# Odd sequences' weighted values in two float32r parts, first pages asked for early, one pipeline for both MLPs, and four branch steps moved to ScalarE

## The chip, the cores and the metric

The kernel runs on one core of a Trainium2 chip. The metric is the device time of one execution in microseconds (us). Engines are called as in the profile: PE (TensorE, the matmuls; PEld are its weight loads), DVE (VectorE), ACT (ScalarE), POOL (GpSimd) and SP (SyncE, which here issues the DMAs).

## The reference, cut to what matters

One inference step of a two-layer decoder with width 1024, for a prompt of 1024 tokens and for 8 sample sequences of 4 new tokens (32 columns), which makes 1056 columns in all. Layer 0 runs two branches side by side, stick-breaking attention of 8 heads and an RG-LRU recurrence over 512 channels. Layer 1 is dilated window attention of 16 heads. Behind each mixer stands a squared-ReLU MLP (1024 to 4096 and back).

```
z = u @ w_in                                   # layer 0: q, k, v, xr, g
attn = stick_breaking(q, [past_k; k], [past_v; v])      # samples: 1024 cached keys, 8 pages of 128
xc = conv_b + sum(conv_w[j] * shifted(xr, j) for j in range(4))
a, inp = gates(xc)                             # sigmoid gates, exp and sqrt(1 - a^2) of 128x1056 tiles
h = scan(a, inp);  lru = gelu(g) * h
x = x + [attn, lru] @ w_out
x = x + square(relu(norm(x) @ w_ff1)) @ w_ff2
```

For a sample sequence b the attention ends in `o[b] = sum over pages of weights(32 x 128) @ values(128 x 512)`: 32 rows are 8 heads by 4 tokens, 512 columns are 8 heads of 64, and of each row only its own head's 64 columns are kept.

## The kernel before, in words

Activations lie transposed, 128 channels by 1056 columns, in 8 tiles. A float32 product is mostly made of float32r parts: `x = xh + xl`, `w = wh + wl`, three matmuls (`mm3`). The high part is an ACT copy, the low part a subtraction on DVE or POOL. Weights pass through `raw_w` (a DMA into one of three `ws` buffers), two ACT copies of half a tile each, and one POOL subtraction.

The stages, in us of the profiled span: loading and turning of x, the branch (`lru_phase`) with its projections up to about 210, layer 0's attention by pairs of heads with the next pair's projections between, from about 430 the sample sequences beside the last pair's attention and an early part of the output projection, from 656 the output projection, the first MLP from 740 to 1470, layer 1's attention to about 2200 and its output projection, the second MLP from 2262 and the final norm.

In the branch, in the rest of layer 0's set-up and in the second MLP a scheduler of the language decides the order. The attention stages are written out by a planner: `interleave` takes the next piece of several generators whose inputs are ready by a model of the engines (`Clock`, `Timed`), in which a DMA is charged by its bytes at 360 GB/s. `after` puts a step (a copy, a subtraction, a DMA) at a planned time. Since helpers record the operations, all ACT, DVE, POOL and SP work has line L138, matmuls L213 and transposes L219; operations are told apart by their tiles.

`sb_samples` (L1436) serves the sample sequences. `fetch` asks for one page of 128 keys or values (256 KB) into one of 18 `u` tiles, and four pages are kept asked for. First 64 key pages are turned on PE (`ktr`), split, and scored. Then `spread` turns the weights into tiles `x` of 128 keys by 32 rows. For each sequence 8 pages and the new keys (`wn`, `vs32`) are summed by plain float32 matmuls of 32 weight columns by 512 value columns; `join` turns the result and copies the kept columns into `ats`. In the profile these products read `tr<-u,x`.

The first MLP (`first_mlp`, L1264) runs 64 units of weights, each loaded four units ahead and split two units ahead, all by hand. The second (`finish_layer`, L1213) writes the same sums plainly, with `last_weights` for its last four tiles, and `last_pass` ends in the final norm.

Of the kernel before, what the change touches and what calls it, by code (L numbers as in the profile page):

```python
# [21 lines left out]
NS = 32  # L22
# [14 lines left out]
def f32(ap):  # L37
    return ap.bitcast(F)
# [89 lines left out]
class Timed:  # L128
# [47 lines left out]
class Trunk:  # L176
# [154 lines left out]

    def parts_w(self, kb, cols, pool=None, bufs=4):
        return [(pool or self.wp).tile([128, kb, cols], R, name=self.nm("w"), tag="w", bufs=bufs) for _ in range(2)]

# [303 lines left out]
    def lru_conv(self, f, xr, oc, T):  # L638
# [19 lines left out]
    def lru_block(self, f, g, xc, bd, sp4, tiny, oc, T):  # L658
# [350 lines left out]
    def layer0(self, st, rstd):  # L1009
# [4 lines left out]
        with self.pool("smp0") as sp, self.pool("qkv0") as qkv:  # L1014
# [7 lines left out]
            with self.pool("pair0") as pool:  # L1022
# [52 lines left out]
                def load_lru(k):  # L1075
# [6 lines left out]
                                 k_step, v_step, T, False, done, 2)  # L1082
                proj = self.projections(st, rstd, win, 512, pps, T)
                self.low_queries(T)
                with self.manual():
                    self.interleave((proj, 1))
                    for p in range(4):
                        self.split_pair(pps[p], T, False)
                        if p == 0:
                            self.after(60000, self.states_out, oc, TS("ot", shape=(36, LRU)), need=[oc])  # L1090
                        if p < 3:
                            self.interleave((att, 106.6 if p else 85.8), (proj, 76))
                    sample = self.sb_samples(smp, pps[3], ats, T, x, load, lambda: first.append(
                        self.out_w(self.i["w_out_ab"][0], range(4), 0, 9000)))
                    early = self.early_out(0, self.i["w_out_ab"][0], ops, range(4, 8),
# [117 lines left out]
    def finish_layer(self, l, ops, wsrc, ks, w):  # L1213
# [7 lines left out]
        with self.pool(f"mlp{l}") as hp:  # L1221
# [9 lines left out]
            nx = {}  # L1231
            if l == 0:
                self.first_mlp(st, rstd, w1, w2, h, nx)
                return nx
            for g in range(8):
                th = [hp.tile([128, NT], R, name=self.nm("th"), tag="th", bufs=6) for _ in range(4)]
                tl = [hp.tile([128, NT], R, name=self.nm("tl"), tag="tl", bufs=6) for _ in range(4)]
                for f in range(4):
                    c0 = (g * 4 + f) * 128
                    w = self.weights(w1[:, :, c0:c0 + 128], 8, 128)  # L1240
                    if g == 7 and f == 3:
                        last = self.last_weights(w2)

                    def ev(ps, s, f=f):
                        t = hp.tile([128, CW], F, name=self.nm("t"), tag="t", bufs=3)
                        q = hp.tile([128, CW], F, name=self.nm("t2"), tag="t2", bufs=3)
                        nc.vector.scalar_tensor_tensor(t, ps, 0.0, rstd[:, s], op0=OP.max, op1=OP.mult)
                        nc.scalar.activation(q, t, AF.Square)
                        nc.scalar.activation(th[f][:, s], q, AF.Copy)
                        nc.vector.tensor_sub(tl[f][:, s], q, f32(th[f][:, s]))  # L1250
                    for _ in self.project(st, w, ev):
                        pass
                if g == 7:
                    self.last_pass(last, th, tl, h)
                    break
                for m2 in range(4):
                    w = self.weights(w2[:, g * 4:g * 4 + 4, m2 * 256:(m2 + 1) * 256], 4, 256)
                    for _ in self.contract(w, (2 * m2, 2 * m2 + 1), range(4), th, tl, h):
                        pass
        return nx  # L1260

    def first_mlp(self, st, rstd, w1, w2, h, nx):  # L1264
        nc, hp = self.nc, self.hp
        todo = self.caches(hp)
        raw, parts = {}, {}
# [27 lines left out]
        load(3)  # L1295
        next(todo)
        with self.tc.manual_schedule(engines={getattr(mybir.EngineType, e) for e in
                                              ("PE", "SP", "Pool", "Activation", "DVE")}):
            for u in range(64):
                g, x = divmod(u, 8)  # L1300
# [7 lines left out]
                if x < 4:  # L1308
                    for c in range(3):
# [15 lines left out]
                        if c < 2:  # L1325
                            cut(u + 2, c)
                    continue
                step = self.norm_done(h, self.g[:, 1], nx) if g == 7 else None
# [18 lines left out]
            for _ in todo:  # L1347
                pass
        self.norm_finish(nx)


    def last_weights(self, w2):
        nc, hp = self.nc, self.hp
        ws = []
        for j in range(4):
            src = w2[:, 28:32, j * 256:(j + 1) * 256]
            if j in (0, 3):
                ws.append(self.weights(src, 4, 256))
                continue
            s, a, b = (hp.tile([128, NT], d, name=self.nm("w"), tag=t, bufs=n)[:, :1024].rearrange(  # L1360
                "p (k f) -> p k f", k=4) for d, t, n in ((F, ("acc", "sq")[j - 1], j), (R, "th", 6), (R, "tl", 6)))
            nc.sync.dma_start(s, src)
            self.split_w(s, a, b)
            ws.append((a, b))
        return ws

# [69 lines left out]
    def sb_samples(self, smp, pp, ats, T, x, load, ahead):  # L1436
# [23 lines left out]
        for _ in range(4):  # L1460
            fetch()
        for t in pp["split_s"]:
            t.run()
# [80 lines left out]
        def spread(half, ready):  # L1544

            yield 0, [ready]
            ready.run()
            ws = [x(t, F, (128, 4, 4, 32)) for t in ("xh", "xl")]
            ws.append(T("wn", shape=(NS, 1, 4, 32), bufs=2))
            for j in range(3):  # L1550
# [6 lines left out]
                nc.scalar.activation(ws[j], ps[:m, :n].rearrange("p k (b r) -> p k b r", b=4), AF.Copy)  # L1557
                self.drop(ps)
                yield 0, 0
            return ws  # L1560

        def join(b, o):

            v = u(F, (32, 512))
            nc.vector.transpose(v, o)
            self.drop(o)
# [28 lines left out]
        for t in pp["vlo"]:  # L1595
            t.run()
        for b in range(8):
            half = b // 4
            yield 0, [TR]
            o = turn([32, 512])  # L1600
            for kb in range(9):
                m = 128 if kb < 8 else NS
                yield 0, [ws[half][kb // 4]] + (here[:1] if kb < 8 else [])
                v = here.pop(0) if kb < 8 else smp["vs32"]
                self.mm(o, ws[half][kb // 4][:m, kb % 4, b % 4], v, start=kb == 0, stop=kb == 8)
                if kb < 8:
                    self.drop(v)
                    fetch()
                    yield 0, 0
                if b * 9 + kb == 12:  # L1610
                    ws[1] = yield from spread(1, ready[1])
# [467 lines left out]
```

## Time and profile before

| what | value |
|---|---|
| median of 3 runs | 3019.85 us (3018.76 to 3021.5) |
| the profiled execution, its own time | 3023.94 us |
| span of its trace | 3022.2 us |
| PE busy in the span | 2873.6 us (95%) |
| DVE, ACT, POOL busy | 1666.2, 1222.1, 952.6 us |
| DMA, mean over the span | 141 GB/s |

The span runs from the first instruction to the last; 1.7 us of the profiled execution lie outside it. PE is busy nearly throughout, so time is to be found where it is idle, where its granted clock is below 1.00, and in matmuls that take long for what they do.

### The profile page before, as it was taken

Reading aid. Unit: us, or ns where it says so; the run is one execution under the profiler, and the core shown is the slowest. Engines: PE = TensorE matmul, PEld = TensorE weight load, DVE = VectorE, ACT = ScalarE, POOL = GpSimd, SP = SyncE. Lnnn points to the kernel's source line nnn. Section 1 sums busy time; section 2 is a strip of 40 time slices with the busy share of each in tenths; the row PEclk is TensorE's granted clock in tenths of the full one; section 3 lists DMA queues with packets and bytes.
Section 4 is the critical chain, followed back from the end, with each engine's and each line's share of the span. In section 5 each row is a group of like instructions: output and inputs, shape, how many; then the busy total and the mean of one; then the engine's idle time right before and its main releaser. Section 6 shows DMA issues by size and latency. Waiting matters only on the chain.

```text
span 3022.2 us, 49205 instructions
## 1 busy us (share of the span) xinstructions
PE 2873.6 (95%) x18608; PEld 2730.8 (90%) x18608; DVE 1666.2 (55%) x3597; ACT 1222.1 (40%) x2441; POOL 952.6 (32%) x591
## 2 busy tenths in 40 slices
PE   7889889999999999999999999998989999999998
PEld 6778879659999999999999989997889999999998
DVE  5877897544444444442467878866663332333335
ACT  4455676434343333332455555544342221212222
POOL 2445562123333333341432222223132121212122
PEclk9999999999999999999999999999989999999999
DMA  5111136664877778861355656566531111111111
GB/s 174 43 50 30 43 106 224 191 211 138 253 247 246 252 252 254 258 222 40 131 185 161 216 160 212 158 221 195 169 128 43 49 43 49 43 49 43 50 36 65
DMA packets 366725, 426.16 MB, mean 141 GB/s; under 512 B 23878, under 2 KB 292822, under 8 KB 366488
## 3 DMA queue, kind: packets, MB, share of 16 engines
q1 hardware_dynamic: 366488, 423.01, 43.7%
q8 instruction: 147, 2.41, 0.3%
q14 instruction: 90, 0.74, 0.1%
HBM read 296.23 MB, written 126.17 MB: 140 GB/s over the span
## 4 chain that ended last, share of the span: by engine, by line
PE 73%; DVE 11%; DMA 4%; ACT 4%; issue 4%; POOL 1%; SPq 1%; ACTq 0%; POOLq 0%; DVEq 0%
PE mm L213 58%; PE tr L213 9%; PE tr L219 3%; PE pv L213 2%; DMA ws<-in_w_in_c_dram 1%; DVE u L138 1%; DVE sa L138 1%; DVE w L138 1%; DVE xl L138 1%; DVE f L138 1%; DVE sb L138 1%; ACT w L138 1%; ACT u L138 1%; DMA U<-kv 1%; DVE tl L138 1%
## 5 line engine op out<-in xcount | busy, mean ns | idle before, releaser
L213 PE MATMUL mm<-xh,w 128*128 128x352 f32 x5184 | 1337.0, 329 | 24.8 <-DVE xr L138 7.1
L213 PEld LDWEIGHTS mm<-xh,w 128*128 128x128 f32 x5184 | 926.7, 191 | 34.8 <-DVE xr L138 8.4
L138 POOL TENSOR_TENSOR w<-ws,w 128x1024 fp32r<-128x1024 f32 (+1 forms) x188 | 464.4, 2471 | 1290.1 <-ACT w L138 1194.5
L213 PE MATMUL mm<-xl,w 128*128 128x352 f32 x2592 | 844.8, 326 | 2.8 <-DVE xl L138 2.8
L213 PE MATMUL mm<-th,w 128*128 128x352 f32 (+2 forms) x3072 | 742.0, 323 | 6.1 <-DVE h L138 6.1
L213 PEld LDWEIGHTS mm<-th,w 128*128 128x128 f32 x3072 | 532.7, 188 | 8.9 <-DVE h L138 8.4
L213 PEld LDWEIGHTS mm<-xl,w 128*128 128x128 f32 x2592 | 495.7, 191 | 6.8 <-DVE xl L138 3.1
L213 PE MATMUL mm<-tl,w 128*128 128x352 f32 (+2 forms) x1536 | 493.3, 321 | 0.0
L138 ACT ACTIVATE w<-ws 128x512 fp32r<-128x512 f32 (+1 forms) x376 | 220.3, 616 | 560.1 <-issue 265.1
L138 DVE TENSOR_TENSOR h<-mm,h 128x352 f32<-128x352 f32 (+2 forms) x384 | 200.3, 523 | 417.4 <-PE mm L213 417.4
L213 PEld LDWEIGHTS mm<-tl,w 128*128 128x128 f32 x1536 | 288.6, 188 | 0.0
L138 ACT ACTIVATE u<-tr 128x512 fp32r<-128x512 f32 (+5 forms) x362 | 188.3, 530 | 189.0 <-PE tr L219 151.5
L138 ACT ACTIVATE t<-t 128x352 f32<-128x352 f32 x192 | 95.2, 496 | 412.4 <-DVE t L138 412.4
L138 DVE TENSOR_TENSOR tl<-t,th 128x352 fp32r<-128x352 f32 x192 | 151.3, 788 | 192.6 <-ACT th L138 192.6
L138 DVE SCALAR_TENSOR_TENSOR t<-mm,rstd 128x352 f32<-128x352 f32 x192 | 100.5, 523 | 281.8 <-PE mm L213 276.9
L138 DVE TENSOR_TENSOR u<-tr,u 128x512 fp32r<-128x512 f32 (+3 forms) x272 | 164.0, 612 | 76.2 <-ACT u L138 73.6
L138 POOL TENSOR_TENSOR kvs<-raw,kvs 128x512 fp32r<-128x512 f32 x80 | 103.0, 1295 | 132.7 <-ACT kvs L138 73.8
L213 PE MATMUL pv<-u,v 128*128 128x256 f32 (+1 forms) x736 | 134.3, 298 | 10.7 <-DVE u L138 10.4
L213 PE MATMUL mm<-x,w 128*128 128x352 f32 x720 | 139.8, 333 | 3.7 <-DVE k L138 2.7
L213 PEld LDWEIGHTS pv<-u,v 128*128 128x128 f32 x736 | 107.3, 197 | 21.4 <-DVE u L138 13.3
L213 PEld LDWEIGHTS mm<-x,w 128*128 128x128 f32 x720 | 117.0, 192 | 10.5 <-issue 4.2
L138 DVE TENSOR_TENSOR_SCAN f<-f,ms 128x128 f32<-128x128 f32 (+3 forms) x64 | 100.4, 1569 | 35.6 <-ACT f L138 35.3
(278 smaller groups left out, 3663.6 us busy)
## 6 DMA issues: line engine op xcount, KB each, us to landing
kv<-kvs SPq DMA_DIRECT2D x160, 512.0 KB
U<-kv SPq DMA_DIRECT2D x160, 512.0 KB
ws<-in_w_ff_dram SPq DMA_DIRECT2D x126, 512.0 KB
raw<-in_cache_dil_k_dram SPq DMA_DIRECT2D x320, 64.0 KB
u<-in_cache_sb_k_dram SPq DMA_DIRECT2D x64, 256.0 KB
u<-in_cache_sb_v_dram SPq DMA_DIRECT2D x64, 256.0 KB
raw<-in_cache_dil_v_dram SPq DMA_DIRECT2D x64, 256.0 KB
out_dram<-u SPq DMA_DIRECT2D x48, 256.0 KB
```

What stands on the lines that cost most here:

```text
L138: r = f(*args, **kw)
L213: self.nc.tensor.matmul(out, w, x, start=start, stop=stop)
L219: self.nc.tensor.transpose(out, x, ident)
```

## The change

Five edits, in the diff below.

1. For sequences 1, 3, 5 and 7 weights and values are split into float32r parts. The weights' high and low parts stand side by side as 64 columns, so two matmuls (high values, low values) give all four partial products in 64 rows. `join` adds the two halves of 32 rows. Per odd page there is one ACT copy and one subtraction (22 of 32 on DVE, 10 on POOL). A value page is prepared one page ahead (`got`). The even sequences and the new keys stay in float32.
2. `sb_samples` is made before the last pair of heads but one, and its first step, the four first page DMAs, is planned 145000 PE cycles into that pair's work.
3. The planner charges a DMA at 230 GB/s in place of 360.
4. Both MLPs run the pipeline of the first (`units`); layer 1 stops it at unit 60 and leaves units 60 to 63 to `last_pass`. `last_weights` is gone.
5. In the branch four steps per block on 128x1056 tiles (`xc`, `ge`, `w`, `e`) go from DVE to ACT.

```diff
-                cost = int(np.prod(o.shape)) * 4 / 360 * 2.4
+                cost = int(np.prod(o.shape)) * 4 / 230 * 2.4
...
-        nc.vector.tensor_scalar(xc, xr, cw[3], V[:, 36:37], op0=OP.mult, op1=OP.add)
+        nc.scalar.activation(xc, xr, AF.Identity, scale=cw[3], bias=V[:, 36:37])
...
-        nc.vector.tensor_scalar(ge, ge, 0.044715, 1.0, op0=OP.mult, op1=OP.add)
+        nc.scalar.activation(ge, ge, AF.Identity, scale=0.044715, bias=1.0)
...
-        nc.vector.tensor_scalar_add(w, u, 1.0)
+        nc.scalar.activation(w, u, AF.Identity, bias=1.0)
...
-        nc.vector.tensor_scalar(e, e, 0.25, -1.0, op0=OP.mult, op1=OP.add)
+        nc.scalar.activation(e, e, AF.Identity, scale=0.25, bias=-1.0)
...
+                        if p == 2:
+                            pages = self.after(145000, next, sample)
...
+                    pages.run()
...
-            for g in range(8):
...
-                    w = self.weights(w1[:, :, c0:c0 + 128], 8, 128)
...
+            self.units(l, st, rstd, w1, w2, h, nx)
...
-                parts[u] = self.parts_w(*raw[u].shape[1:], *((hp, 2) if u % 3 == 2 else ()))
+                where = (hp, 4, "wl") if l and u > 61 else (hp, 2) if u % 3 == 2 else ()
+                parts[u] = self.parts_w(*raw[u].shape[1:], *where)
...
-            for u in range(64):
+            for u in range(60 if l else 64):
...
+                    hi, lo = (ws[j][1][..., c:c + 32] for c in (0, 32))
+                    nc.scalar.activation(ws[j][0], src[:, :, 0::2], AF.Copy)
+                    nc.scalar.activation(hi, src[:, :, 1::2], AF.Copy)
+                    lows.append(self.after(300, nc.vector.tensor_sub, lo, src[:, :, 1::2], f32(hi), drops=[ps]))
...
+        def value(n):
+
+            t = here.pop(0)
+            if n // 8 % 2 == 0:
+                return (t,)
+            vh, vl = u(), u()
+            nc.scalar.activation(vh, t, AF.Copy)
+            return vh, vl, self.after(300, (nc.gpsimd if n % 3 == 1 else nc.vector).tensor_sub, vl, t, f32(vh), drops=[t])
...
+            if b % 2:
+                t = u(F, (32, 512))
+                nc.scalar.activation(t, o[32:64], AF.Copy)
+                nc.vector.tensor_add(t, o[0:32], t)
+                nc.vector.transpose(v, t)
...
-                self.mm(o, ws[half][kb // 4][:m, kb % 4, b % 4], v, start=kb == 0, stop=kb == 8)
...
+                if len(v) == 1:
+                    yield 0, [w[kb // 4][0]]
+                    self.mm(o[0:32], lw, v[0], start=n == 0, stop=n == 8)
+                    self.drop(*v)
+                else:
+                    yield 0, [v[2], lows[kb // 4]]
+                    for t in (v[2], lows[kb // 4]):
+                        t.run()
+                    self.mm(o, lw, v[0], start=n == 0, stop=False)
+                    self.mm(o, lw, v[1], start=False, stop=n == 8)
+                    self.drop(*v[:2])
```

DVE's queue in the branch, at the second half of its first block (tiles `w_876`, `e_877`, `a_871`), where the third block's `xr_900` is taken out of PE's banks. Before:

```order
L138 TENSOR_TENSOR xr_900<-mm_909,rstd_290 128x352
L138 TENSOR_SCALAR w_876<-u_849 128x1056
L138 SCALAR_TENSOR_TENSOR e_877<-a_871,w_876 128x1056
L138 TENSOR_TENSOR xr_900<-mm_935,rstd_290 128x352
L138 TENSOR_SCALAR e_877<-e_877 128x1056
L138 TENSOR_TENSOR w_876<-u_849,z_872 128x1056
L138 SCALAR_TENSOR_TENSOR e_877<-a_871,e_877 128x1056
L138 TENSOR_TENSOR z_872<-w_876,z_872 128x1056
L138 TENSOR_TENSOR a_871<-u_849,e_877 128x1056
L138 SCALAR_TENSOR_TENSOR w_876<-z_872,w_876 128x1056
L138 TENSOR_TENSOR xr_900<-mm_961,rstd_290 128x352
```

And now:

```order
L138 TENSOR_TENSOR xr_900<-mm_909,rstd_290 128x352
L138 TENSOR_TENSOR xr_900<-mm_935,rstd_290 128x352
L138 SCALAR_TENSOR_TENSOR e_877<-a_871,w_876 128x1056
L138 TENSOR_TENSOR xr_900<-mm_961,rstd_290 128x352
L138 TENSOR_TENSOR w_876<-u_849,z_872 128x1056
L138 SCALAR_TENSOR_TENSOR e_877<-a_871,e_877 128x1056
L138 TENSOR_TENSOR z_872<-w_876,z_872 128x1056
```

Two steps are gone from the queue, and between the second and the last `xr` stands one long step of the block where six stood before. The second `e` step now waits for a step on ACT.

PE's queue in the value products. Before, in the middle of them (`kb`, `qb`, `sa`, `pv` belong to the last pair's attention):

```order
L213 MATMUL tr_7343<-kb_4091,ql_199_1451 128x512
L213 MATMUL tr_7212<-vs_194_1440,wn_6071 32x512
L213 MATMUL tr_7357<-u_7285,x_6968 32x512
L213 MATMUL tr_7357<-u_7330,x_6968 32x512
L213 MATMUL tr_7357<-u_7336,x_6968 32x512
L219 MATMUL tr_7415<-ident,sa_6966 128x128
L219 MATMUL tr_7415<-ident,sa_7034 128x128 x2
L213 MATMUL tr_7357<-u_7339,x_6968 32x512
L213 MATMUL tr_7357<-u_7364,x_6969 32x512
L213 MATMUL pv_7207<-u_7191,v_1406_5180 128x256
```

Now, where the fourth sequence ends (two rows per odd page) and the fifth begins:

```order
L213 MATMUL tr_7628<-u_7705,x_6152 64x512
L213 MATMUL tr_7628<-u_7706,x_6152 64x512
L213 MATMUL tr_7628<-u_7751,x_6152 64x512
L213 MATMUL tr_7628<-u_7752,x_6152 64x512
L213 MATMUL tr_7628<-vs_194_1440,wn_6153 32x512
L213 MATMUL tr_7628<-u_7759,x_6152 64x512
L213 MATMUL tr_7628<-u_7760,x_6152 64x512
L213 MATMUL tr_7783<-u_7708,wp_7387 32x512
L213 MATMUL tr_7783<-u_7754,wp_7387 32x512
```

The planner has moved the last pair's attention and the early output projection ahead: from the third sequence's second page on, 47 of the 64 value pages follow each other with nothing of the attention between, only the new keys' products, and in the eighth sequence 20 rows of the output projection.

ACT's queue in the second MLP, where the fourth tile of the first group of hidden channels (`th_25912` before, `th_26118` now) is made in three thirds. Before:

```order
L138 ACTIVATE t_6766_26318<-t_26317 128x352
L138 ACTIVATE th_25912<-t_6766_26318 128x352
L138 ACTIVATE w_26447<-ws_26445 128x512 x2
L138 ACTIVATE t_6769_26349<-t_26348 128x352
L138 ACTIVATE th_25912<-t_6769_26349 128x352
```

And now:

```order
L138 ACTIVATE th_26118<-t_6928_26486 128x352
L138 ACTIVATE w_26491<-ws_26258 128x512
L138 ACTIVATE t_6933_26520<-t_26519 128x352
L138 ACTIVATE th_26118<-t_6933_26520 128x352
L138 ACTIVATE w_26491<-ws_26258 128x512
L138 ACTIVATE t_6936_26553<-t_26552 128x352
L138 ACTIVATE th_26118<-t_6936_26553 128x352
```

The two half copies of a weight tile, after which POOL subtracts, stood together ahead of the last third; now one stands behind each of the first two thirds, and the tile is that of two units later.

## Rows read from the trace of the kernel before

**Rows 1.** Stages: window, PE, PEld, DVE, ACT, POOL busy (count), clock, DMA share, GB/s
```profile
97.00:210.00 113.00, 89.67 (x450) 82.30 (x449) 96.89 (x89) 50.87 (x63) 48.70 (x26) 0.89 0.10 34
...
430.00:450.00 20.00, 9.18 (x79) 8.46 (x78) 18.90 (x23) 12.95 (x23) 17.08 (x18) 0.74 0.93 308
...
568.00:656.00 88.00, 87.61 (x257) 26.10 (x255) 36.25 (x70) 26.54 (x49) 16.14 (x15) 1.00 0.69 219
...
740.00:1470.00 730.00, 730.00 (x4556) 729.58 (x4555) 309.84 (x546) 265.29 (x491) 268.29 (x148) 1.00 0.68 219
1470.00:2262.00 792.00, 744.17 (x5292) 701.13 (x5291) 570.52 (x1859) 392.37 (x907) 220.06 (x141) 0.96 0.56 180
2262.00:2990.00 728.00, 721.94 (x4494) 718.15 (x4493) 251.72 (x423) 172.83 (x335) 158.60 (x72) 1.00 0.15 45
```

**Rows 2.** Waits of PE in 97:210, us in total, times, longest
```profile
PE mm L213 <- DVE xr L138: 7.1, 2, 3.7
PE mm L213 <- DVE k L138: 6.4, 2, 5.0
PE mm L213 <- DVE q L138: 3.9, 1, 3.9
PE mm L213 <- DVE g L138: 3.0, 1, 3.0
```

**Rows 3.** Groups of DVE and ACT in 97:210: busy us, mean ns, idle before
```profile
L138 DVE TENSOR_SCALAR w<-u 128x1056 f32<-128x1056 f32 x4 | 6.8, 1688 | 11.7 <-ACT u L138 11.7
...
L138 DVE TENSOR_SCALAR e<-e 128x1056 f32<-128x1056 f32 x4 | 2.8, 701 | 0.0
...
L138 DVE TENSOR_SCALAR xc<-xr,vec 128x1056 f32<-128x1056 f32 x2 | 1.6, 818 | 0.0
...
L138 DVE TENSOR_SCALAR ge<-ge 128x1056 f32<-128x1056 f32 x2 | 1.4, 703 | 0.0
...
L138 ACT ACTIVATE a<-a 128x1056 f32<-128x1056 f32 x4 | 4.3, 1082 | 11.9 <-DVE a L138 11.9
```

**Rows 4.** Timeline at 441: start, us, engine, operation, idle before and its releaser
```profile
441.43 2.48 DVE L138 TENSOR_TENSOR u<-tr,u 128x512 fp32r<-128x512 f32 x4
...
442.22 1.09 PE L219 MATMUL tr<-ident,u 128*128 128x128 f32 x4 [7.63 <-DMA u<-in_cache_sb_k_dram]
```

**Rows 5.** Timeline of PE among the value products; two records are one float32 product
```profile
606.62 2.76 PE L213 MATMUL tr<-u,x 128*32 128x512 f32 x6
609.32 0.50 PE L213 MATMUL tr<-kb,qb 128*128 128x512 f32 x1
609.65 0.40 PE L213 MATMUL tr<-kb,ql 128*128 128x512 f32 x1
609.98 0.61 PE L213 MATMUL tr<-vs,wn 32*32 32x512 f32 x1
```

**Rows 6.** Copies and subtractions of 128x512 tiles in 568:656
```profile
L138 POOL TENSOR_TENSOR x<-u,x 128x512 fp32r<-128x512 f32 x4 | 5.0, 1276 | 18.9 <-ACT x L138 18.9
...
L138 ACT ACTIVATE x<-u 128x512 fp32r<-128x512 f32 x6 | 3.7, 625 | 3.4 <-DMA u<-mix 3.3
...
L138 DVE TENSOR_TENSOR x<-u,x 128x512 fp32r<-128x512 f32 x2 | 1.3, 687 | 0.0
```

**Rows 7.** The fullest ten us of transfers among the value products
```profile
610.00:620.00 10.00, 10.00 (x29) 2.90 (x29) 4.89 (x9) 4.57 (x9) 1.94 (x2) 1.00 0.90 298
```

**Rows 8.** The second MLP, 2262:2990: PE's waits for the sum's evacuation
```profile
PE mm L213 <- DVE h L138: 4.7, 7, 0.9
```

**Rows 9.** Timeline at one of these waits
```profile
2301.45 1.15 ACT L138 ACTIVATE w<-ws 128x512 fp32r<-128x512 f32 x2 [2.14 <-PE mm L213]
...
2302.74 2.40 POOL L138 TENSOR_TENSOR w<-ws,w 128x1024 fp32r<-128x1024 f32 x1 [9.17 <-ACT w L138]
...
2303.56 1.96 DVE L138 TENSOR_TENSOR tl<-t,th 128x352 fp32r<-128x352 f32 x1 [1.47 <-ACT th L138]
```

**Rows 10.** The same subtraction in the first MLP, where POOL rests
```profile
832.86 0.53 DVE L138 TENSOR_TENSOR tl<-t,th 128x352 fp32r<-128x352 f32 x1 [0.48 <-ACT th L138]
```

More of the change, by code (lines that the diff above doesn't have):

```diff
@@ L330, in raw_w, with parts_w @@
         return s
-    def parts_w(self, kb, cols, pool=None, bufs=4):
-        return [(pool or self.wp).tile([128, kb, cols], R, name=self.nm("w"), tag="w", bufs=bufs) for _ in range(2)]
+    def parts_w(self, kb, cols, pool=None, bufs=4, tag="w"):
+        return [(pool or self.wp).tile([128, kb, cols], R, name=self.nm("w"), tag=tag, bufs=bufs) for _ in range(2)]
     def split_w(self, s, h, l):
@@ L1083, in layer0 @@
                 proj = self.projections(st, rstd, win, 512, pps, T)
+                sample = self.sb_samples(smp, pps[3], ats, T, x, load, lambda: first.append(
+                    self.out_w(self.i["w_out_ab"][0], range(4), 0, 9000)))
                 self.low_queries(T)
@@ L1090, in layer0 @@
                             self.after(60000, self.states_out, oc, TS("ot", shape=(36, LRU)), need=[oc])
+                        if p == 2:
+                            pages = self.after(145000, next, sample)
                         if p < 3:
                             self.interleave((att, 106.6 if p else 85.8), (proj, 76))
-                    sample = self.sb_samples(smp, pps[3], ats, T, x, load, lambda: first.append(
-                        self.out_w(self.i["w_out_ab"][0], range(4), 0, 9000)))
+                    pages.run()
                     early = self.early_out(0, self.i["w_out_ab"][0], ops, range(4, 8),
@@ L1231, in finish_layer, with units @@
             nx = {}
-            if l == 0:
-                self.first_mlp(st, rstd, w1, w2, h, nx)
-                return nx
-            for g in range(8):
[L1236 to L1239, printed above, removed]
-                    w = self.weights(w1[:, :, c0:c0 + 128], 8, 128)
[L1241 to L1259, printed above, removed]
+            self.units(l, st, rstd, w1, w2, h, nx)
         return nx
-    def first_mlp(self, st, rstd, w1, w2, h, nx):
+    def units(self, l, st, rstd, w1, w2, h, nx):
         nc, hp = self.nc, self.hp
-        todo = self.caches(hp)
+        todo = iter(()) if l else self.caches(hp)
         raw, parts = {}, {}
@@ L1295, in first_mlp @@
         load(3)
-        next(todo)
+        next(todo, None)
         with self.tc.manual_schedule(engines={getattr(mybir.EngineType, e) for e in
                                               ("PE", "SP", "Pool", "Activation", "DVE")}):
-            for u in range(64):
+            for u in range(60 if l else 64):
                 g, x = divmod(u, 8)
@@ L1326, in first_mlp @@
                             cut(u + 2, c)
+                    if l and u == 59:
+                        for v in (62, 63):
+                            cut(v, 0)
+                            cut(v, 1)
                     continue
@@ L1348, in first_mlp @@
                 pass
[L1349 to L1365, printed above, removed]
+        if l:
+            self.last_pass([parts[u] for u in range(60, 64)], th, tl, h)
+        else:
+            self.norm_finish(nx)
     def last_pass(self, ws, th, tl, h):
@@ L1461, in sb_samples @@
             fetch()
+        yield 0, 0
         for t in pp["split_s"]:
@@ L1547, in spread @@
             ready.run()
-            ws = [x(t, F, (128, 4, 4, 32)) for t in ("xh", "xl")]
+            ws = [(T("wp", shape=(128, 4, 2, 32), bufs=4), x(t, R, (128, 4, 2, 64))) for t in ("xh", "xl")]
             ws.append(T("wn", shape=(NS, 1, 4, 32), bufs=2))
+            lows = []
             for j in range(3):
@@ L1596, in sb_samples @@
             t.run()
+        got = []
         for b in range(8):
@@ L1599, in sb_samples @@
             yield 0, [TR]
[L1600 to L1604, printed above, removed]
-                self.mm(o, ws[half][kb // 4][:m, kb % 4, b % 4], v, start=kb == 0, stop=kb == 8)
[L1606 to L1610, printed above, removed]
+            o = turn([64, 512])
+            for n, kb in enumerate((0, 1, 2, 3, 4, 5, 6, 8, 7)):
+                w, lows = ws[half]
+                if kb == 8:
+                    self.mm(o[0:32], w[2][:, 0, b % 4], smp["vs32"], start=False, stop=False)
+                    continue
+                k = b * 8 + kb
+                if not got:
+                    yield 0, here[:1]
+                    got.append(value(k))
+                if k < 63:
+                    yield 0, here[:1] + ([("u", 2)] if (k + 1) // 8 % 2 else [])
+                    got.append(value(k + 1))
+                fetch()
+                v = got.pop(0)
+                lw = w[kb // 4][b % 2][:, kb % 4, b % 4 // 2]
+                if len(v) == 1:
+                    yield 0, [w[kb // 4][0]]
+                    self.mm(o[0:32], lw, v[0], start=n == 0, stop=n == 8)
+                    self.drop(*v)
+                else:
+                    yield 0, [v[2], lows[kb // 4]]
[4 more added lines that the diff above has]
+                    self.drop(*v[:2])
+                yield 0, 0
+                if k == 11:
                     ws[1] = yield from spread(1, ready[1])
```

13 lines of the change are left out of this document (9 added, 4 removed).

## The prediction

> **What bounds the kernel now.** I read the stages' busy times first, then PE's waits in those where PE is not full, then the queues it waits for. The first MLP keeps PE busy for all of its 730 us at full clock, 4556 matmuls of 352 columns, 0.160 us each [rows 1]. That is what a stage looks like when only fewer or shorter matmuls can help. The others differ from it in three ways. In the branch, 97 to 210, PE is idle for 23.3 of 113 us and its clock is granted at 0.89 (below 1.00 means stretches at 1.2 instead of 2.4 GHz, here beside the idle ones), while DVE is busy for 96.9 [rows 1]. Four waits for DVE, 7.1, 6.4, 3.9 and 3.0 us, make 20.4 of the idle time [rows 2]: PE's banks are full and the step that empties them stands in DVE's queue behind the block's long steps. Among the value products, 568 to 656, PE is full, so there the price of a product counts; and transfers run at 219 GB/s [rows 1]. In the second MLP PE is idle for 6.1 of 728 us, 4.7 of it in seven waits for DVE [rows 1, 8]. Layer 1's attention has 47.8 us of idle time, spread out, and DVE at 72% [rows 1].
>
> **The branch.** Sixteen steps leave DVE; in the window they are worth 6.8 + 2.8 + 1.6 + 1.4 = 12.6 us [rows 3]. ACT takes about 1.08 us for such a step (the row a<-a is one) [rows 3], so 16 x 1.08 = 17 us go into a queue that is busy for 51 of 113 us [rows 1]. Since 20.4 of PE's 23.3 idle us are waits for DVE, 12.6 x 20.4 / 23.3 = 11 us come back if ACT answers at once. It does not quite: the chain through a block now crosses from DVE to ACT and back twice more, and may find another such step ahead of it. I take 2 us for that, because other DVE work stands ready in the changed queue: -9 us. The bounds: all idle time goes (-23), or each of the eight new crossings costs a step and one ahead of it, 8 x 2.2 = 17 us, with nothing gained.
>
> The Trainium skill (Trainium Architecture — The Big Picture, "The five engines, in one table") says that ScalarE is not for simple arithmetic, where VectorE is up to about three times faster per element. The trace agrees in direction, 0.70 against 1.08 us for the step e; by that rule alone the term would be 16 x 0.38 = 6 us lost, which is what the second rival comes to where DVE is not the bound.
>
> **The first pages.** PE waits for the first key page for 7.63 us [rows 4]. Asked for ahead of the third pair's last two stores, it should have landed. But little is won: DVE is busy for 18.9 of these 20 us [rows 1] and gets to the four attention and page subtractions only at 441.43, 0.8 us before PE goes on [rows 4]. The first scores need them, so DVE is late next. I take -2 us; bounds -7.6, and +2 if four held tiles of 18 delay the attention before.
>
> **The value products.** A float32 product takes (609.32 - 606.62) / 3 = 0.90 us [rows 5]. An odd page has two float32r products of 512 columns instead. Their price is not shown for 64 weight columns; from above it is the 0.33 us between the two attention products among the float32 ones [rows 5], from below 0.160 x 512 / 352 = 0.233 us from the MLP's pace [rows 1]. So a page takes 0.47 to 0.66 us, and 32 pages save 7.7 to 13.9 us. I take 13.9, since in the changed order these products mostly follow each other, as in the MLP.
>
> Then the transfers come due. 47 pages now stand without the attention between them. PE needs 23 x 0.90 + 24 x 0.47 + 6 x 0.90 (new keys) + 20 x 0.16 (output projection) = 40.6 us for them. The transfers: 47 pages of 0.262 MB less four asked for ahead, 11.3 MB, plus six half tiles of the mixed heads and two weight tiles behind the same queue, 2.6 MB, so 13.9 MB. At the fullest ten us of this stage, 298 GB/s at a share of 0.90 [rows 7], that is 46.6 us, 6 more than PE needs. I take 8, since with four pages asked for ahead an odd sequence, used up in 4 us, outruns the queue. Bounds: 1 us at 331 GB/s (308 over its share of 0.93 [rows 1]), 23 at the stage's present 219 GB/s. The stage's sum is -13.9 + 8 = -6; from -13 to +15. ACT copies (0.63 us) and subtractions (0.69 on DVE, 1.28 on POOL [rows 6]) lie beside it: 20, 15 and 13 us on engines now busy for 27, 36 and 16 of 88 [rows 1]. If that cover fails, it is the third rival.
>
> **The second MLP.** The waits come once per group of hidden channels. ACT makes two weight halves (1.15 us) ahead of the last third of th, POOL's subtraction starts at 2302.74 and ends at 2305.14, and DVE's subtraction beside it takes 1.96 us [rows 9], where the same one takes 0.53 with POOL at rest [rows 10]; the sum's evacuation stands behind it. In `units` POOL starts one third earlier, and the first MLP, with the same code and more work beside it, shows no wait at all [rows 1]. So -4.7 us; bounds -6.1 (all idle time) and +2 if the last four weight tiles, split together, delay the last pass. PE's own order here is the same.
>
> **What only moves.** The planner's new DMA price reorders both attention stages. PE's work in them is unchanged, and no row says which way a new order errs, so I take 0, from -8 to +8.
>
> **The sum.** -9 - 2 - 6 - 4.7 = -21.7 us, on the profiled execution's 3023.94 us: 3002 us. The three runs' median is 4.1 us below that execution, so 2998 us is what I forecast, in the terms of 3019.85.
>
> **Rivals.** First, the transfers keep up (331 GB/s or more) and the value stage gives 13 instead of 6: 2991 us. For it speaks that a DMA share of 1 is not reached in it now; against it, the four-page depth.
>
> Second, the branch gives nothing: DVE waits where it worked before, since it already waits 11.7 us for ACT's u ahead of the step w [rows 3], and that step is moved behind the same u on ACT. Then 2998 + 9 = 3007 us. Against it speaks the changed order, with PE's banks emptied two steps apart instead of eight.
>
> Third, slower: an odd page goes through a chain, landing, ACT's copy (0.63), a subtraction (0.69 on DVE, 1.28 on POOL), two products (0.47), and is prepared only one page ahead. If these do not overlap, a page takes 1.8 to 2.4 us instead of 0.90, and 32 pages lose 29 to 48 us where I have 6 gained: about 38 - 15.7 = +22, 3042 us. It decides from the point at which an odd page takes 0.90 + 15.7 / 32 = 1.4 us. For it: 10 of the 32 subtractions are on POOL, and a DVE step stretches beside POOL (1.96 against 0.53 [rows 9, 10]). Against: the engines' queues let page k+1 be copied while page k is multiplied.
>
> The Trainium skill (SBUF — State Buffer, "Summary: rules for kernel authors") says that a DVE operation with two SBUF inputs and a GpSimd operation that reads SBUF block each other for the whole instruction; the trace's 1.96 us agrees. By it the subtractions of neighbouring pages would go one after the other, which is this rival's way of happening.
>
> Fourth, the new order costs: if half of the 47.8 us that PE now idles in layer 1's attention [rows 1] came on top, 24 us, the time would be 3022. There DVE is fuller than the transfers (72% against 56%), and the DMA price does not touch DVE, so I see no direction.
>
> **How the numbers follow.** Chances: the forecast 0.43, the first rival 0.22, the second 0.20, the third 0.07, the fourth 0.08. What a measurement of this kernel can tell from no change is about 0.2%, 6 us. Faster than 3013.8: nearly all of the first three cases (0.41, 0.22, 0.17) and a little of the fourth, 0.82. Within: 0.02 + 0.03 and half of the fourth, 0.09. Slower: the third and some of the fourth, 0.09. The range goes from 2982 (the first rival with the branch at -18) to 3014 (the second rival with the value stage at +1).
>
> **What would show it.** In the branch PE's waits for xr, g, q and k shrink from 20 us to under 10. The wait of 7.6 us for the first key page is gone and DVE, not a DMA, precedes the first scores. The value products show 64 float32 records less, 64 new ones at about 0.23 us, and waits for value pages of 5 to 12 us in all. The second MLP's seven waits for DVE are gone. I am wrong if PE waits for DVE's or POOL's low parts of values, if the branch's end moves by less than 4 us, or if layer 1's attention changes by more than 8.

## The result and the profile after

The changed kernel takes 3000.87 us (median of 5 runs, 3000.59 to 3006.68) against 3020.06 us; the ratio is 0.994, 95% interval 0.9929 to 0.9951. The profiled execution took 3000.87 us, its span 2999.1. That lies near the forecast of 2998, but the 23.1 us by which the span fell came from other places than forecast. First and last instructions of the stages, in us of the two spans:

| instruction | before | after | shift |
|---|---|---|---|
| first attention scores `tr<-ka,qa` | 221.9 | 218.8 | -3.1 |
| first `mm<-th` of the first MLP | 781.3 | 777.8 | -3.5 |
| first `mx` of layer 1's attention | 1529.0 | 1526.7 | -2.3 |
| last `mx` there | 2200.3 | 2186.6 | -13.7 |
| `tr<-ones,acc` ahead of the second MLP | 2248.7 | 2232.5 | -16.2 |
| last `mm<-th` of the second MLP | 3011.8 | 2988.2 | -23.6 |

All of layer 0 up to its MLP gave 3.5 us, where I had 17. Layer 1's attention, where I had 0, gave 11.4. From `tr<-ones` to the last `th` it was 7.4. The stages after, in the columns of [rows 1]:

```profile
97.00:210.00 113.00, 88.02 (x453) 81.16 (x452) 88.93 (x82) 60.46 (x72) 46.50 (x26) 0.88 0.10 33
430.00:450.00 20.00, 14.17 (x129) 13.16 (x130) 17.91 (x22) 11.60 (x19) 17.42 (x17) 0.83 0.86 275
580.00:669.00 89.00, 77.41 (x265) 31.02 (x263) 58.99 (x90) 39.12 (x72) 28.76 (x19) 0.92 0.71 227
737.00:1467.00 730.00, 730.00 (x4552) 729.51 (x4551) 309.83 (x546) 264.34 (x489) 267.85 (x147) 1.00 0.68 219
1467.00:2248.00 781.00, 736.62 (x5299) 692.36 (x5297) 565.47 (x1861) 394.88 (x912) 218.67 (x141) 0.97 0.56 181
2248.00:2970.00 722.00, 721.98 (x4510) 720.37 (x4510) 207.44 (x427) 170.96 (x332) 159.86 (x74) 1.00 0.15 47
```

The branch has 8.0 us less of DVE and 9.6 more of ACT, but PE is idle for 25.0 us, where it was 23.3. Among the value products PE, which was full, is idle for 11.6 of 89 us, and its granted clock fell to 0.92. The second MLP lost its idle time, as forecast.

In the branch the waits changed place [rows 2]. PE's waits from 97 to the first scores, in us, times, longest:

```profile
PE tr L213 <- issue: 7.7, 1, 7.7
PE mm L213 <- DVE q L138: 6.2, 1, 6.2
PE mm L213 <- DVE k L138: 3.9, 1, 3.9
PE mm L213 <- DVE g L138: 3.2, 1, 3.2
PE mm L213 <- DVE xr L138: 2.6, 1, 2.6
PE tr L213 <- ACT u L138: 1.6, 2, 1.4
```

The waits named for DVE fell from 20.4 to 15.9 us, but the first row was 2.6 us before (`PE tr L213 <- issue: 2.6, 1, 2.6`). The timeline of PE and of DVE shows what it is:

```profile
119.51 2.69 PE L213 MATMUL tr<-xc,lru_wa 128*128 128x352 f32 x4 [7.66 <-issue]
```

```profile
118.16 1.25 DVE L138 SCALAR_TENSOR_TENSOR xc<-xr,vec,xc 128x1021 f32<-128x1021 f32 x1
```

The second block's gate products start 0.1 us after DVE's last long step on their `xc` ends (118.16 + 1.25), so this is DVE's queue again. Before, that step ran from 119.41 to 120.68: `xr` is now emptied some 9 us earlier (the last third at 100.34 instead of 109.58), but `xc`, behind the first block's steps, is ready only 1.3 us earlier, so PE reaches this point sooner and waits there. PE's waits come to 25.2 us against 23.2.

The first key page is no longer awaited from a DMA [rows 4], but from DVE:

```profile
433.52 1.12 PE L219 MATMUL tr<-ident,u 128*128 128x128 f32 x4 [5.56 <-DVE u L138]
```

Among the value products PE waits for low parts (580 to 669), and the subtractions on pages take longer than in [rows 6]. The waits come first; the groups then give busy us, mean ns, and the idle time before them:

```profile
PE tr L213 <- DVE u L138: 7.0, 8, 2.5
PE tr L213 <- ACT u L138: 1.7, 1, 1.7
PE tr L213 <- POOL w L138: 1.4, 1, 1.4
PE tr L213 <- POOL u L138: 1.4, 2, 0.7
```

```profile
L138 DVE TENSOR_TENSOR u<-u,u 128x512 fp32r<-128x512 f32 x22 | 25.8, 1208 | 11.2 <-ACT u L138 11.0
L138 ACT ACTIVATE u<-u 128x512 fp32r<-128x512 f32 x32 | 19.2, 624 | 18.6 <-DMA u<-in_cache_sb_v_dram 13.9 <-PE tr L213 3.2 <-DVE u L138 1.2
L138 POOL TENSOR_TENSOR u<-u,u 128x512 fp32r<-128x512 f32 x10 | 14.3, 1439 | 41.4 <-ACT u L138 21.9 <-DVE u L138 13.5 <-PE tr L213 6.1
```

A subtraction takes 1.21 us on DVE in the mean where 0.69 was shown before: thirteen of the 22 still take 0.64 to 0.69 us, and nine, each beside an operation on POOL, take 1.35 to 2.86. ACT waits 13.9 us for pages to land, so the chain starts late as well as running slowly.

### The profile page after: what moved, and what is told of

It reads as the page before. It is cut to its first block, busy times and chain, and to the rows that moved or that the text cites. A ratio compares the mean times of both kernels' runs of the same rounds, so it can differ in the third digit from the quotient of the medians.

```text
span 2999.1 us, 49338 instructions
## 1 busy us (share of the span) xinstructions
PE 2852.8 (95%) x18608; PEld 2725.0 (91%) x18608; DVE 1624.7 (54%) x3611; ACT 1256.5 (42%) x2496; POOL 960.1 (32%) x601
## 4 chain that ended last, share of the span: by engine, by line
PE 69%; DVE 4%; ACT 2%; DMA 1%; issue 1%; POOL 0%; SPq 0%; ACTq 0%; DVEq 0%; POOLq 0%
PE mm L213 58%; PE tr L213 7%; PE tr L219 2%; PE pv L213 2%; DVE sa L138 1%; DVE sb L138 1%; DVE u L138 1%; DMA U<-kv 0%; DMA mix<-o 0%; DVE mx L138 0%; DVE xl L138 0%; ACT u L138 0%; ACT xh L138 0%; ACT w L138 0%; POOL acc L138 0%
## 5 line engine op out<-in xcount | busy, mean ns | idle before, releaser
L213 PE MATMUL mm<-xh,w 128*128 128x352 f32 x5184 | 1325.7, 328 | 17.2 <-DVE q L138 6.8
L213 PEld LDWEIGHTS mm<-xh,w 128*128 128x128 f32 x5184 | 922.0, 190 | 24.8 <-DVE q L138 7.4
L213 PE MATMUL mm<-xl,w 128*128 128x352 f32 x2592 | 841.8, 325 | 0.0
L213 PE MATMUL mm<-th,w 128*128 128x352 f32 (+2 forms) x3072 | 739.6, 323 | 0.0
L213 PEld LDWEIGHTS mm<-th,w 128*128 128x128 f32 x3072 | 532.3, 188 | 0.7
L213 PEld LDWEIGHTS mm<-xl,w 128*128 128x128 f32 x2592 | 493.5, 190 | 3.5 <-issue 0.2
L213 PE MATMUL mm<-tl,w 128*128 128x352 f32 (+2 forms) x1536 | 493.0, 321 | 0.0
L213 PEld LDWEIGHTS mm<-tl,w 128*128 128x128 f32 x1536 | 288.6, 188 | 0.0
L138 ACT ACTIVATE u<-tr 128x512 fp32r<-128x512 f32 (+6 forms) x366 | 190.8, 531 | 218.8 <-PE tr L219 182.1
L138 DVE TENSOR_TENSOR tl<-t,th 128x352 fp32r<-128x352 f32 x192 | 103.5, 539 | 181.5 <-ACT th L138 181.5
L138 DVE TENSOR_TENSOR u<-tr,u 128x512 fp32r<-128x512 f32 (+4 forms) x276 | 166.4, 613 | 62.5 <-ACT u L138 58.0
L213 PE MATMUL pv<-u,v 128*128 128x256 f32 (+1 forms) x736 | 134.0, 298 | 8.9 <-DVE u L138 8.7
L213 PE MATMUL mm<-x,w 128*128 128x352 f32 x720 | 137.4, 334 | 5.0 <-DVE k L138 3.5
L213 PEld LDWEIGHTS mm<-x,w 128*128 128x128 f32 x720 | 118.4, 193 | 8.2 <-DVE k L138 4.4
L213 PEld LDWEIGHTS pv<-u,v 128*128 128x128 f32 x736 | 105.3, 194 | 14.8 <-DVE u L138 11.2
L138 DVE TENSOR_TENSOR_SCAN f<-f,ms 128x128 f32<-128x128 f32 (+3 forms) x64 | 102.3, 1601 | 11.6 <-ACT f L138 11.3
```

The source lines that it names most:

```text
L213: self.nc.tensor.matmul(out, w, x, start=start, stop=stop)
```

## The experiments

My theory from the two traces was: the planner's price of a DMA made layer 1's attention shorter; the split values gained nothing, because pages land or are split too slowly; the branch steps gave about 3 us. Each median below is that of 5 to 12 runs.

| kernel | price | median us | ratio to before, 95% |
|---|---|---|---|
| changed, price back | 360 | 3018.99 | 0.9981 to 1.0002 |
| before, price alone | 230 | 2999.39 | 0.9914 to 0.9945 |
| before, pipeline for both MLPs alone | 360 | 3014.20 | 0.9968 to 0.9990 |
| that, and price | 290 | 3014.69 | 0.9970 to 0.9987 |
| that, and price | 230 | 2995.16 | 0.9901 to 0.9927 |
| that, and price | 180 | 3043.07 | 1.0054 to 1.0078 |
| that at 230, and split values | 230 | 2999.14 | 0.9908 to 0.9933 |
| changed, branch steps on DVE | 230 | 3000.99 | 0.9906 to 0.9942 |
| changed, float32 values | 230 | 2999.92 | 0.9904 to 0.9939 |
| changed, no subtraction of values | 230 | 2996.25 | 0.9899 to 0.9933 |
| changed, all subtractions on DVE | 230 | 2999.24 | 0.9910 to 0.9942 |
| changed, eight pages ahead | 230 | 3001.98 | 0.9921 to 0.9951 |

**The price of a DMA.** Four kernels change this line alone, to the value named with each; the last two start from the kernel with the price at 230 and the one pipeline:

```diff
-                cost = int(np.prod(o.shape)) * 4 / 230 * 2.4
+                cost = int(np.prod(o.shape)) * 4 / 360 * 2.4
```

Back in the changed kernel:

> The changed kernel with the planner's DMA price back at 360. Theory: the price alone made layer 1's attention 11 us shorter (no other edit touches it), and in layer 0 it moved the attention ahead of the value products and so took their cover. Then layer 1's attention (first mx to last mx) goes back from 660 to about 671 us, the value stage gets shorter by 3 to 8 us, and the total is 3004 to 3009 us. Rival: the price decides little, layer 1 was shortened by the state in which the earlier edits leave the queues; then its attention stays at 660 us and the total is within 3 us of 3001.

Alone in the kernel before (360 to 230):

> The kernel before with only the planner's DMA price at 230. Theory: the price alone gives the changed kernel most of its gain, in layer 1's attention (11 to 14 us by the first and the last mx there), so 3005 to 3008 us. Rival: the price works only together with the other edits (price back alone took 18 us from the changed kernel, but without the others it need not give them): 3013 us or more.

At 290 and at 180:

> The kernel of the first run of this set with the price at 290 in place of 230. Theory: the gain grows as the price comes nearer to what the transfers take beside the attention (180 to 230 GB/s in the trace), so between the two: 2995 to 3008 us. Rival: the price only picks one of several orders and 290 has either the old result or the new: 3012 to 3016 us, or 2989 to 2994 us.

> The same with the price at 180. Theory: 230 is near the truth and a still dearer price plans the work too late: 2994 to 3005 us. Rival: the dearer the better, 2980 to 2988 us.

Price back cost the changed kernel 18.1 us, more than the theory had; the price alone gave the kernel before 20.6 us, more than expected too and at least as much as all five edits together (19.2). Layer 1's attention went back as expected. The value stage didn't get shorter: at 360 PE is still idle for 11.5 of the 80 us from 600, and the last value product comes at 673.5 us, so it isn't the price that opened the stall there. The expectations for 290 and 180 both missed: 290 has the old result, as its rival said, and 180 is slower than anything named. From first to last `mx`, layer 1's attention takes 671.3, 671.8 and 669.6 us in the three kernels at 360, 678.0 at 290, 654.4 to 662.6 in the nine at 230, and 704.0 at 180. So the price decides there, and a dearer price is not simply a better one: 290 gained nothing in total (it reaches the first MLP 7.9 us earlier than the same kernel at 360, and loses 8.4 in this stretch), 180 lost 48 us against 230. Rows of that stretch in the kernel before, with the price alone, and at 180 (columns of [rows 1]):

```profile
1529.00:2200.30 671.30, 638.04 (x4683) 598.28 (x4682) 507.03 (x1760) 336.35 (x808) 164.73 (x112) 0.98 0.58 186
```

```profile
1517.80:2178.70 660.90, 636.56 (x4682) 595.47 (x4681) 501.23 (x1759) 336.59 (x807) 163.04 (x112) 0.98 0.59 189
```

```profile
1527.20:2231.20 704.00, 650.93 (x4681) 607.48 (x4680) 505.26 (x1758) 335.32 (x807) 162.88 (x112) 0.97 0.55 178
```

The work is the same, PE's idle time is 33.3, 24.3 and 53.1 us; at 180 its busy time also grew by 13 us, at a granted clock of 0.97. At 230 two waits shrank by 14.0 us together, and others grew. PE's longest waits in that stretch before, and with the price alone:

```profile
PE tr L219 <- DVE mx L138: 12.8, 6, 5.3
PE tr L219 <- DVE tl L138: 5.6, 1, 5.6
```

```profile
PE tr L213 <- DVE u L138: 5.7, 14, 0.8
PE tr L219 <- DVE mx L138: 4.4, 4, 2.4
```

The longest wait for `mx` is 2.4 us instead of 5.3, and that for `tl`, the softmax of the last sample's scores, is gone. PE's timeline shows how, before and with the price alone (`mm<-x,w` is the early part of the output projection):

```profile
2116.95 0.62 PE L219 MATMUL tr<-ident,sb 128*128 128x128 f32 x4
2123.13 0.87 PE L219 MATMUL tr<-ident,tl 64*128 64x64 f32 x6 [5.56 <-DVE tl L138]
```

```profile
2107.22 4.08 PE L213 MATMUL mm<-x,w 128*128 128x352 f32 x24
...
2118.52 0.65 PE L213 MATMUL mm<-x,w 128*128 128x352 f32 x3
2119.10 0.58 PE L219 MATMUL tr<-ident,tl 64*128 64x64 f32 x6
```

With DMAs priced dearer the planner puts matmuls of the output projection between the scores and the turning of `tl`, so PE has them while DVE and ACT work at the softmax; at 360 nothing stands there. At 180 waits for DVE's `mx`, `u` and `q` come back all over the stretch.

This is about half of what the price gave; the rest came in layer 0. With the price alone the first `mm<-th` of the first MLP comes at 769.7 us instead of 781.3, and PE's idle time from 220 us to it falls from 44.4 to 35.0; in the pair with the one pipeline it comes at 775.0 instead of 779.8 (43.5 and 39.1 us idle). So its part there is somewhere from 5 to 12 us. The planner's order in layer 0 differs too, and which of its waits the price took isn't shown here.

**The branch.** The sixteen steps, four per block, back on DVE; one of the four:

```diff
-        nc.scalar.activation(w, u, AF.Identity, bias=1.0)
+        nc.vector.tensor_scalar_add(w, u, 1.0)
```

> The changed kernel with the branch's sixteen steps back on DVE. Theory by the milestones of the two traces: the steps are worth the 3.2 us by which the first attention scores come earlier, so 3004 us. Rival 1: they are also the cause of the further 3.8 us by the end of the pairs of heads: 3008 us. Rival 2, the forecast's own term: 9 us, 3010 us.

3000.99 against 3000.87 us: the steps are worth nothing that can be measured. All three expectations fall. The first scores come at 218.8 to 221.3 us in the six kernels with ACT's steps (mean 220.0) and at 220.3 to 221.9 in the eight without (221.1).

**The value products.** Plain float32 products as before; then the split without its subtractions (the high part is taken twice and the low parts are left out, so PE's work is the same); then all of these on DVE; then more pages ahead:

> The changed kernel with all value products in plain float32 as before (pages still asked for early, price 230). Theory: the split's own chain (landing, copy, subtraction, products) eats what the shorter products give, so the total stays within 4 us of 3001 us, at either side. Rival 1: the split is worth its 6 to 14 us and the new order lost more than that around it: 3007 to 3015 us. Rival 2: the split costs: 2990 to 2997 us.

```diff
-            vh, vl = u(), u()
+            vh = u()
...
-            return vh, vl, self.after(300, (nc.gpsimd if n % 3 == 1 else nc.vector).tensor_sub, vl, t, f32(vh), drops=[t])
+            self.drop(t)
+            return vh, vh
...
```

> The changed kernel without the 32 subtractions that make the low parts of the odd value pages; the second product of such a page takes the high part again, so PE's work is the same. Theory: the low part's chain (copy, then a subtraction beside others on DVE and POOL) makes PE wait, and the 14 us of idle time that the split adds there go: 2987 to 2993 us. Rival: the pages land no faster than the present pace, and only the cause named by PE changes: 2998 to 3004 us.

```diff
-            return vh, vl, self.after(300, (nc.gpsimd if n % 3 == 1 else nc.vector).tensor_sub, vl, t, f32(vh), drops=[t])
+            return vh, vl, self.after(300, nc.vector.tensor_sub, vl, t, f32(vh), drops=[t])
```

> The changed kernel with all 32 subtractions of value pages on DVE, none on POOL. Theory: what stretches the chain is DVE and POOL side by side (DVE's subtractions took 1.6 us beside POOL, 0.69 alone): 2994 to 2998 us. Rival 1: DVE's own queue decides, and 10 more steps of 0.7 us in it cost up to 7 us: 3003 to 3008 us. Rival 2: the pages' landing decides: within 3 us of 3001 us.

```diff
                 fetch()
+                if 18 <= k < 22:
+                    yield 0, [("u", 1)]
+                    fetch()
```

> The changed kernel with eight value pages asked for ahead instead of four, from the third sequence's third page on. Theory of the landing: odd sequences outrun four pages, so 5 to 12 us go: 2989 to 2996 us. Rival, the chain of copy and subtraction, which is one page ahead in both: within 3 us of 3001 us.

The stage from 600 to 680 in the changed kernel, with float32 values, and without subtractions (columns of [rows 1]):

```profile
600.00:680.00 80.00, 65.87 (x211) 27.45 (x211) 46.24 (x79) 30.93 (x59) 23.60 (x15) 0.89 0.78 259
```

```profile
600.00:680.00 80.00, 80.00 (x292) 35.32 (x291) 29.44 (x62) 19.99 (x38) 15.40 (x9) 1.00 0.70 233
```

```profile
600.00:680.00 80.00, 68.72 (x243) 31.72 (x242) 26.82 (x64) 30.62 (x58) 10.27 (x6) 0.94 0.81 273
```

With float32 values PE is full, with the split it is idle for 14.1 us. These 80 us don't hold the same work in both, since the planner puts parts of the output projection before 600 when there is the split. So here are PE's product rows of both (those of the changed kernel first, even and odd pages), and both kernels from 220 us to the first MLP:

```profile
L213 PE MATMUL tr<-u,wp 128*32 128x512 f32 x64 | 32.0, 636 | 0.0
L213 PE MATMUL tr<-u,x 128*64 128x512 f32 x64 | 23.5, 455 | 10.2 <-DVE u L138 7.0 <-ACT u L138 1.7 <-POOL u L138 1.4
```

```profile
L213 PE MATMUL tr<-u,x 128*32 128x512 f32 x128 | 61.9, 599 | 0.0
```

```profile
220.00:777.80 557.80, 505.88 (x3384) 441.86 (x3384) 407.75 (x565) 321.34 (x619) 235.49 (x174) 0.96 0.44 141
```

```profile
220.00:777.40 557.40, 517.61 (x3393) 438.90 (x3392) 381.37 (x537) 303.54 (x583) 224.13 (x164) 0.97 0.45 141
```

The products take 55.5 us in place of 61.9, and all of PE's work up to the first MLP is 11.7 us less, but PE is idle for 12.1 us more. The last value product comes at 670.2 us in the one and 669.9 in the other, and the total is the same, as the theory had it. The low parts alone are not the cause: without them PE is still idle for 11.3 us, now waiting for pages and their copies, and the total is 4.6 us lower with intervals that overlap, between the theory's range and the rival's. All subtractions on DVE leave 11.2 us (1.6 us less in total), eight pages ahead 13.3 us (1.1 more); in both the rival held, within 3 us. So no one of chain, POOL or depth sets the pace alone.

SP's requests for pages show one more limit, close behind these. In the kernel without subtractions (start, us, operation; then the page indices that SP loads):

```profile
628.21 13.37 SPq L138 DMA_DIRECT2D u<-in_cache_sb_v_dram  x16
```

```profile
631.89 2.04 SPq L138 DMA_DIRECT2D u<-in_cache_sb_v_dram  x4
```

```profile
L1422 SPq TENSOR_LOAD <-pt x19: 295/299/580, 541.0 to 650.4; - x19
```

SP asks for four pages in 2.04 us. Then it loads the next four page indices from the page table (0.30 us) and works them into addresses, and the next four requests start 3.64 us after these (631.89 and 635.53). In these 13.37 us its waits come to 0.6 us. From 599.5 to 654.6 it asks for 48 pages, and its waits come to 9.4 of 55.1 us. In all fourteen traces no two such loads among the value pages stand closer than 3.63 us. So SP cannot ask for pages faster than one in 0.91 us, whatever the transfers do. PE took 0.90 us for a float32 page [rows 5]: where value pages follow each other, a faster product has next to nothing to win. No run here made SP's part shorter, so how much of PE's idle time is its share isn't shown; in the changed kernel SP also waits 6.8 us for PE's products from 604 to 658.7.

**The pipeline of the second MLP, and what adds up.** The kernel before with `units` for both MLPs; the same at 230; and that with split values:

```diff
-            if l == 0:
-                self.first_mlp(st, rstd, w1, w2, h, nx)
...
+            self.units(l, st, rstd, w1, w2, h, nx)
```

> The kernel before with only the second MLP changed to the pipeline of the first. Theory by the traces' ends (second MLP 8 to 10 us shorter): 3010 to 3012 us. Rival, the forecast's term: only the seven waits of 4.7 us go, 3015 us; what went beyond it in the changed kernel then came from the start of the stage, which the layer 1 attention decides.

> The kernel before with the planner's DMA price at 230 and the one pipeline for both MLPs, nothing else: no split values, no early pages, no branch steps. Theory: the price's 20 us and the 8 us that the second MLP took less in every kernel with the pipeline add up, 2989 to 2994 us, and this beats the changed kernel; the other three edits together then cost it some 8 us. Rival: the gains do not add, since whatever layer 0 wins is lost again in layer 1: 2997 to 3002 us.

> The same with the split values, which is the changed kernel without the early pages and the branch steps. Theory: with the price at 230 the early pages cost 5 to 8 us in layer 0 and the split nothing, so 2988 to 2995 us, within 3 us of the kernel above. Rival 1: the split is what costs: 2997 to 3003 us. Rival 2: without the early pages the split gives its 6 us: 2980 to 2987 us.

The pipeline gives 5.8 us at 360, where the rival's 3015 us was nearer than the theory, and 4.2 at 230 (3020.0 to 3014.2, 2999.4 to 2995.2); the second pair's intervals overlap. PE's longest waits from `tr<-ones` to the last `th`, with the price alone and with price and pipeline:

```profile
PE mm L213 <- DVE h L138: 4.6, 7, 0.7
PE tr L213 <- DVE acc L138: 1.9, 1, 1.9
```

```profile
PE tr L213 <- DVE acc L138: 6.2, 1, 6.2
```

The seven waits are gone; at the start of the stage PE now waits longer for the norm's sum, which gives part of it back. Price and pipeline alone make the fastest kernel, 2995.16 us (2992.58 to 3000.97), 5.7 below the changed one. So the split, the early pages and the branch steps together cost about 5 us: 3000.9 against 2995.2 at 230, where the intervals are apart, and 3019.0 against 3014.2 at 360, where they overlap by a little. Which of them costs it isn't settled. The split added 4.0 us without the early pages, as its first rival had it, and 1.0 with them, and the intervals of such pairs overlap. The kernels with the price alone and with price and pipeline have the same order on PE up to the second MLP, yet reach the first MLP at 769.7 and 775.0 us, so single profiles of layer 0 say nothing below some 5 us.

## Why the prediction was right, and where it was wrong

The time was right by two errors that cancel, which is luck: the price, put at 0, gave 18 to 21 us, and the three edits of layer 0, put at 17 together, cost about 5. Only the second MLP's term was right by its mechanism.

- **What only moves** ("no row says which way a new order errs, so I take 0, from -8 to +8") is the step that failed most. My reason was that the price doesn't touch DVE, which is fuller than the transfers. But it moves PE's spare work beside DVE's chains, and [rows 1] held 47.8 us of idle time to be covered. The fourth rival had the size, 24 us, with the wrong sign for this price; at 180 something like it came about (idle time from 33.3 to 53.1 us).
- **The branch**, -9: nothing. The second rival was right in the outcome. The waits for `xr` shrank as forecast, from 7.1 to 2.6 us, but the wait for `xc` in the same queue grew from 2.6 to 7.7: the chain through a block sets the pace, not DVE's sum. DVE's busy time fell by 8.0 us instead of 12.6, since other steps of it took longer (`a<-u,e` 9.5 us in all, where it was 5.0), and ACT's rose by 9.6 in this window, not by 17.
- **The first pages**, -2: "DVE is late next" held, 5.56 us of the 7.63 remained. What it gave in total was not measured alone; with the two edits around it, it lies in the 5 us that are lost.
- **The value products**, -6: the saving was put at 13.9 us, and the products' rows show 6.4 (61.9 to 55.5); without the subtractions they show 10.0 (51.9). In the changed kernel PE worked at a granted clock of 0.50 from 622.3 to 636.0, which the float32 kernel didn't. The stall that I put at 8 us was 12 to 14. The stage as a whole gave nothing: within my bounds (-13 to +15), but the wrong value. I let the transfers set the pace at the fullest ten us of before (298 GB/s) and never counted SP's own instructions: 0.91 us a page is 288 GB/s for pages at best, with every other request on top, and the stage ran at 259. I also took copies and subtractions as hidden; where they ran beside POOL they were part of the stall. The third rival's price of 1.4 us a page was not reached: the stage got no longer.
- **The second MLP**, -4.7: right, 4.2 and 5.8 us by the medians, and the waits named are the ones that went.

Of what I said would prove me wrong, all three came: waits for low parts of values, a branch end that moved by 3.1 us, and layer 1's attention by 11.4.

The Trainium skill (SBUF — State Buffer, "Summary: rules for kernel authors") says to estimate end-to-end time between HBM and SBUF with about 358 GB/s. No run here tests that figure as a rate. As the planner's price 360 was the worse choice (3020.0 us against 2999.4 with 230), but 290 and 180 were worse than 230 too, so these times rank orders of work, not rates; the stages move 180 to 219 GB/s [rows 1].

The Trainium skill says in the same section that a DVE operation with two SBUF inputs and a GpSimd operation that reads SBUF block each other. The nine stretched subtractions agree (1.35 to 2.86 us, each beside an operation on POOL, against 0.69), but taking POOL's ten away changed the time by 1.6 us only, with 11.2 us of PE's idle time left: these subtractions were not the only thing that PE waited for.

## What to carry to other kernels

A constant in a planner that looks like a model of the hardware is a choice of order: give it a term and a range as wide as the idle time that order could cover, and try a few values, since 290, 230 and 180 gave 3014.7, 2995.2 and 3043.1 us. A shorter matmul pays only down to the pace at which its operand arrives, so compare that pace, the issuing queue's own instructions included, with the matmul's old time (here 0.91 and 0.90 us a page) before counting the saving. When the total agrees, still compare stage by stage: here one edit of five carried most of the result, a second gave 4 to 6 us, and leaving the other three out is faster.

## What the runs showed of the hardware that I had not expected

A 128x512 subtraction on DVE took 1.21 us in the mean and up to 2.86, on POOL 1.44, where 0.69 and 1.28 were shown before [rows 6]. In the branch DVE's product `w<-w,ah` on 128x8 took 2.38 us beside a POOL product (`ig<-ig,xc`, from 112.65 to 115.78), where the same step took 0.16 in the kernel before; it stands in the queue ahead of `xc`. The wait shows as busy time of the step, not as idle time before it.

While PE waited among the value products its granted clock fell, in the changed kernel to 0.50, which is 1.2 GHz, from 622.3 to 636.0; from 617 to 622.7 it had been idle four times, for 0.28 to 1.65 us. In the float32 kernel, where PE is full, it stayed at 1.00:

```profile
622.30:636.00 13.70, 12.41 (x19) 2.99 (x20) 8.77 (x12) 4.53 (x9) 4.88 (x3) 0.50 0.86 275
```

SP spent 0.91 us a page on requests whose addresses come from a table: 2.04 us on four requests, 1.6 on loading and working up the next four indices.
